# A shared PSUM bank in the gated-linear-attention scan: keys in halves of it, products in the attention's ring

## The chip, the cores and the metric

The kernel runs on one core of a Trainium2 chip. The metric is the device time of one execution in microseconds (us); lower is better.

## The reference, cut to what matters

A two-layer backbone over 1280 tokens (256 context, then 1024 latent) of width 1024. Each layer normalises its input, multiplies it by one input projection, runs three groups of heads on the result and adds one output projection of them all:

```python
for layer in range(DEPTH):            # DEPTH = 2
    p = h @ w_in                      # one combined input projection
    gdn = gdn_branch(...)             # gated DeltaNet, a scan over chunks
    mla = mla_branch(...)             # softmax attention, 8 heads, 96-wide keys
    gla = gla_branch(...)             # gated linear attention, a scan over chunks
    x = x + gate * (concat([gdn, mla, gla]) @ w_out)
```

The change sits in the last branch, the gated linear attention (GLA), in its recurrence over chunks, run once forward and once backward over the tokens:

```python
o = (qi * jnp.exp(bi)) @ state + scores @ vi
state = state * jnp.exp(b_last)[..., None] + einsum(ki * jnp.exp(b_last - bi), vi)
```

## The kernel before, in words

The kernel is one program in the Tile language. It is written as a sequence of instructions; a planner of the language then lists each engine's instructions in an order that it works out with a timeline of its own (`schedule_with_timeline_sim=True`), gives tiles their buffers and adds the waits. A pool with `bufs=n` has n buffers for a tag: a new tile takes one whose earlier tile has been read for the last time, and its first writer waits for that reader.

In each layer, after the projections, `run` starts two strands of work and interleaves them. The foreground is first `up` (the attention's queries, keys and values), then `attend`. The background is a generator: the scan of the gated DeltaNet (`gdn_scan`), then `gla_prep`, seven levels `gla_level` and at last `gla_scan`. After each step of the foreground one step of the background is written.

`attend` works in units: one tile of 128 queries against all 1280 keys of one head. Scores go to tiles `sa` (two banks each, two buffers) and `sb`; ScalarE takes exponentials; ten 128x128 transposes (`ptr`, L1243) bring the probabilities into tiles of the tag `t`, four, four and two at a time, and ScalarE or VectorE copies each to SBUF (L1247). For each group of four units `output` multiplies with the values into a tile `O` (40 matmuls, L1255, and four with the reciprocal sums, L1267), also of the tag `t`, and VectorE reads it (L1269, L1271). The tag `t` has two buffers, each a PSUM bank: this is the attention's ring.

The background has one PSUM bank of its own, tag `l`, one buffer. The helper that hands out both:

```python
def g(self, name="g", tag="g"):
    if tag == "l":
        return self.psl.tile([128, 512], F32, name=name, tag=tag, bufs=1)
    return self.ps.tile([128, 512], F32, name=name, tag=tag, bufs=self.psb[tag])
```

`gla_scan` has ten stages `st`, each with both directions `d`. A stage transposes two 128x128 key tiles into a tile `kdt` (L950), which ScalarE copies to `ktl` (L952); multiplies queries with the state and the scores with the values into `gO` (L961, L964), which ScalarE or VectorE brings to `oL` (L973, L975); and multiplies the keys with the values into `gF` (L980), from which VectorE makes the new state `Sl` with a mask (L982) and the decayed old state (L988). `kdt` and `gF` exist in the first nine stages of each layer; `gO` in all ten of the first layer and in eight of the second, which needs no output for the context: 18 tiles of each name in all. `Sl` and `ktl` have two buffers. After stages 1, 7 and 9 `head_norm` norms and gates finished outputs and writes them to DRAM (`y_d`, L1009).

When the background is done its SBUF pools close, and `proj_start` lays its pool `yC` over the same memory: it loads the attention's output (`yst`, L1316) and the first output weights (`wost`, L248, split by L249 and L250 with one staging buffer), makes gate tiles (L1331, tag `l`) and transposes the scans' outputs (`ytr`, L1350). `proj` then loads the other weights over the attention's memory and runs the output projection (`po`).

Of the kernel before, what the change touches and what calls it, by code (L numbers as in the profile page):

```python
# [43 lines left out]
class Net:  # L44
# [25 lines left out]

    def S(self, name="S"):
        return self.ps.tile([128, 1536], F32, name=name, tag="S", bufs=self.psb["S"])

# [130 lines left out]
    def h_stage(self, l, a, b):  # L204
# [17 lines left out]
        for k in range(8):  # L222
            if k % 2 == 0:
                pp = self.S("hps")
            ps = pp[:, 512 * (k % 2):512 * (k % 2) + w]
# [33 lines left out]
    def chan(self, w, j, lo=0):  # L259

        hi, lw = (t.rearrange("p (k n) -> p k n", k=8) for t in w)
        ps = self.S("pin")
        for c0, cn in CHUNKS:
# [419 lines left out]
    def gdn_scan(self, l):  # L683
# [7 lines left out]
        oS = sp.tile([128, 20 * 256], F32, name="oS", tag="oS", bufs=1)  # L691
        S = None
        lanes = [(d, h) for h in range(4) for d in range(2)]
# [7 lines left out]
        for s in range(20):  # L701
# [23 lines left out]
            r = vt  # L725
            if S is not None:
                pk = self.g("kS", "l")
# [198 lines left out]
    def gla_scan(self, l):  # L926
        nc, sp = self.nc, self.sp
        last = l == L - 1
        mm = nc.tensor.matmul
        V, A, P = nc.vector, nc.scalar, nc.gpsimd  # L930
        Q, K, tot = (self.lst[n] for n in ("Q", "K", "tots"))

        def at(i):

            return self.A5[i // 2][:, 512 * (i % 2):512 * (i % 2) + 512]

        oL = [self.bp.tile([128, 512], F32, name="oL", tag="oL", bufs=5) for _ in range(5)]
        order = (tuple(range(10)), (1, 0) + tuple(range(9, 1, -1)))
        S = [None, None]
        for st in range(10):  # L940
            vs, kt = [], None
            for d in range(2):
                vv = sp.tile([128, 256], F32, name="gvt", tag="gvt", bufs=4)
                nc.sync.dma_start(vv, self.gv_d[l][order[d][st]])
                vs.append(vv)
            if st < 9:
                pk = self.g("kdt", "l")
                for d in range(2):
                    i = order[d][st]
                    nc.tensor.transpose(pk[:, 128 * d:128 * d + 128], K[d][:, 128 * i:128 * i + 128], self.ident)  # L950
                kt = sp.tile([128, 256], F32, name="ktl", tag="ktl", bufs=2)
                A.copy(kt, pk[:, 0:256])  # L952
                yield
            todo = [d for d in range(2) if not (last and order[d][st] < CT) and (d == 0 or S[d] is not None)]
            if todo:
                ps = self.g("gO", "l")
                for d in todo:
                    i = order[d][st]
                    pd = ps[:, 256 * d:256 * d + 256]
                    if S[d] is not None:  # L960
                        mm(pd, Q[d][:, 128 * i:128 * i + 128], S[d], start=True, stop=(d == 1))  # L961
                    if d == 0:
                        for hd in range(4):
                            mm(pd[:, 64 * hd:64 * hd + 64], at(i)[:, 128 * hd:128 * hd + 128], vs[0][:, 64 * hd:64 * hd + 64],  # L964
                               start=(S[d] is None), stop=(S[d] is None or hd == 3))
                for d in todo:
                    i = order[d][st]
                    o = oL[i // 2][:, 256 * (i % 2):256 * (i % 2) + 256]
                    pd = ps[:, 256 * d:256 * d + 256]

                    other = (1 - i if i < 2 else 11 - i) if d == 0 else i
                    if st < other or (d == 0 and i == 1):
                        A.copy(o, pd)  # L973
                    else:
                        V.tensor_tensor(o, pd, o, ALU.add)  # L975
                yield
            if st < 9:
                pf = self.g("gF", "l")
                for d in range(2):
                    mm(pf[:, 256 * d:256 * d + 256], kt[:, 128 * d:128 * d + 128], vs[d], start=True, stop=True)  # L980
                Sn = sp.tile([128, 512], F32, name="Sl", tag="Sl", bufs=2)
                V.tensor_tensor(Sn.rearrange("p (d n) -> p d n", d=2), pf.rearrange("p (d n) -> p d n", d=2),  # L982
                                self.bdm.unsqueeze(1).broadcast_to([128, 2, 256]), ALU.mult)
                for d in range(2):
                    Sd = Sn[:, 256 * d:256 * d + 256]
                    if S[d] is not None:
                        i = order[d][st]
                        V.scalar_tensor_tensor(Sd, S[d], tot[:, d, i:i + 1], Sd, ALU.mult, ALU.add)  # L988
                    S[d] = Sd
            for j in {1: (0,), 7: (2, 3), 9: (1, 4)}.get(st, ()):  # L990
                self.head_norm(l, 1, oL[j], j)
            yield
# [591 lines left out]
```

## Time and profile before

| | us |
|---|---|
| runs shown: lowest, median, highest of 3 | 2273.74, 2279.19, 2281.04 |
| the profiled execution, its own time | 2280.18 |
| its span, first to last instruction | 2278.4 |
| mean granted TensorE clock | 0.946 of full |

The first layer's attention begins some 640 us into the span and its GLA scan some 954 us; in the second layer the scan begins some 2043 us. PE is TensorE's matmuls, DVE is VectorE, ACT is ScalarE, POOL is GpSimd, SPq is SyncE's queue of DMA issues.

### The profile page before, as it was taken

The page shows a single profiled execution, that of the slowest core. Times are in us where ns is not written, and L with a number is a line of the kernel's source. Part 1 is how long each engine was busy: PE and PEld are TensorE (multiplying, and loading weights), DVE is VectorE, ACT ScalarE, POOL GpSimd, SP SyncE. Part 2 cuts the span into 40 slices and gives each one's busy share as a digit, 9 for nine tenths or more (in the row PEclk, how much of TensorE's full clock was granted, in tenths as well). Part 3 has the DMA queues.
Part 4 walks back from the last instruction along what each step waited for, and adds up shares of the span by engine and source line. Part 5 has one row for each costly group of instructions (what it writes and reads, how often), then busy time and mean ns, then how long its engine had stood idle before and what let it go on. Part 6 is the DMA issues. An engine that isn't in the chain of part 4 may idle for free.

```text
span 2278.4 us, 44490 instructions
## 1 busy us (share of the span) xinstructions
PE 2043.3 (90%) x17820; PEld 1709.8 (75%) x17820; DVE 1291.6 (57%) x2187; ACT 941.1 (41%) x1926; POOL 743.7 (33%) x936
## 2 busy tenths in 40 slices
PE   5998997999989988898897998976987999899998
PEld 3987896886767766676897987875876776667688
DVE  3446685323447689656425356795233677975634
ACT  3246311533235466555204356212542445564531
POOL 1233265122234543214103322381123264421410
PEclk8999998899989999999898999998998999899999
DMA  7111343258742231113424212424266242101352
GB/s 296 47 62 61 105 119 113 84 200 284 220 109 76 76 111 36 40 48 121 161 93 171 65 36 81 136 69 115 90 197 168 58 115 96 54 24 50 100 155 103
DMA packets 207551, 247.34 MB, mean 109 GB/s; under 512 B 60976, under 2 KB 164464, under 8 KB 203760
## 3 DMA queue, kind: packets, MB, share of 16 engines
q1 hardware_dynamic: 207344, 244.49, 34.1%
q8 instruction: 140, 2.29, 0.4%
q14 instruction: 67, 0.55, 0.1%
HBM read 168.14 MB, written 76.28 MB: 107 GB/s over the span
## 4 chain that ended last, share of the span: by engine, by line
PE 46%; DVE 13%; ACT 5%; DMA 5%; issue 3%; POOL 2%; SPq 1%; DVEq 0%; POOLq 0%; ACTq 0%
PE O L1255 6%; PE ptr L1243 4%; PE po L257 3%; PE po L255 3%; PE po L256 3%; PE sa L255 3%; PE sa L256 2%; PE sa L257 2%; PE ptk L255 1%; PE ptk L256 1%; PE ptk L257 1%; DVE XT L634 1%; DVE X L636 1%; PE kS L730 1%; DVE acc L345 1%
## 5 line engine op out<-in xcount | busy, mean ns | idle before, releaser
L255 PE MATMUL ptk<-whi,hhi 128*128 128x256 f32 (+1 forms) x912 | 263.6, 290 | 6.1 <-DVE ev L297 2.2
L257 PE MATMUL ptk<-whi,hlo 128*128 128x256 f32 (+1 forms) x912 | 261.9, 288 | 1.8 <-POOL hlo L238 1.7
L256 PE MATMUL ptk<-wlo,hhi 128*128 128x256 f32 (+1 forms) x912 | 261.7, 287 | 0.4 <-DVE wlo L250 0.4
L1243 PE MATMUL ptr<-c_id,P 128*128 128x128 f32 x1312 | 203.6, 283 | 27.8 <-ACT PT L1247 18.8
L1243 PEld LDWEIGHTS ptr<-c_id,P 128*128 128x128 f32 x1312 | 151.2, 143 | 78.1 <-ACT PT L1247 29.9
L1247 ACT COPY PT<-ptr 128x512 f32<-128x512 f32 (+1 forms) x256 | 122.3, 480 | 211.1 <-PE ptr L1243 209.7
L256 PE MATMUL pin<-hlo,whi 128*128 128x512 f32 (+1 forms) x544 | 201.6, 371 | 1.6 <-issue 1.6
L255 PE MATMUL pin<-hhi,whi 128*128 128x512 f32 (+1 forms) x544 | 202.5, 372 | 0.0
L257 PE MATMUL pin<-hhi,wlo 128*128 128x512 f32 (+1 forms) x544 | 201.8, 372 | 0.0
L255 PEld LDWEIGHTS ptk<-whi,hhi 128*128 128x128 f32 x912 | 179.4, 197 | 10.8 <-issue 4.3
L1206 DVE TENSOR_REDUCE mx<-sa 128x1 f32<-128x1024 f32 x128 | 156.2, 1220 | 53.6 <-PE sa L257 53.0
L257 PEld LDWEIGHTS ptk<-whi,hlo 128*128 128x128 f32 x912 | 178.8, 197 | 5.3 <-POOL hlo L238 3.0
L256 PEld LDWEIGHTS ptk<-wlo,hhi 128*128 128x128 f32 x912 | 179.4, 197 | 3.1 <-issue 2.0
L1255 PE MATMUL O<-PT,vv 128*64 128x256 f32 x1312 | 169.6, 388 | 1.7 <-ACT PT L1247 0.9
L255 PE MATMUL po<-wohi,yh 128*128 128x256 f32 x576 | 164.4, 286 | 4.4 <-DVE yl L1353 2.1
L256 PE MATMUL po<-wolo,yh 128*128 128x256 f32 x576 | 164.0, 285 | 0.0
L257 PE MATMUL po<-wohi,yl 128*128 128x256 f32 x576 | 162.6, 285 | 0.0
L1228 ACT ACTIVATE P<-sa,mx 128x1024 f32<-128x1024 f32 x128 | 142.2, 1111 | 0.0
L1255 PEld LDWEIGHTS O<-PT,vv 128*64 128x64 f32 x1312 | 97.2, 138 | 59.0 <-issue 11.9
L255 PE MATMUL sa<-kTh,qTh 128*128 128x512 f32 (+1 forms) x272 | 118.3, 436 | 21.1 <-ACT kTh L1152 15.2
L250 POOL TENSOR_TENSOR wlo<-wst,whi 128x1024 fp32r<-128x1024 f32 x32 | 84.1, 2639 | 127.5 <-ACT whi L249 126.4
L256 PEld LDWEIGHTS pin<-hlo,whi 128*128 128x128 f32 x544 | 105.6, 194 | 19.7 <-issue 4.4
(341 smaller groups left out, 5030.6 us busy)
## 6 DMA issues: line engine op xcount, KB each, us to landing
wada<-in_w_ada_dram SPq DMA_DIRECT2D x24, 1024.0 KB
wst<-in_w_in_dram SPq DMA_DIRECT2D x48, 512.0 KB
kv<-ktv_d SPq DMA_DIRECT2D x80, 128.0 KB
wost<-in_w_out_dram SPq DMA_DIRECT2D x16, 512.0 KB
xt<-in_x_all_dram SPq DMA_DIRECT2D x10, 512.0 KB
at_d<-D SPq DMA_DIRECT2D x4, 1280.0 KB
kn_d<-uo SPq DMA_DIRECT2D x20, 256.0 KB
v_d<-uo SPq DMA_DIRECT2D x20, 256.0 KB
```

The lines of the kernel that those rows point to most:

```text
L250: E.tensor_tensor(lo[:, h], st, hi[:, h].bitcast(F32), ALU.subtract)
L255: mm(out, lh, rh, start=first, stop=False)
L256: mm(out, lh, rl, start=False, stop=False)
L257: mm(out, ll, rh, start=False, stop=last)
L345: nc.vector.scalar_tensor_tensor(a, raw[:, tap:tap + 1282], cw[:, ti, tap:tap + 1], a, ALU.mult, ALU.add)
L634: E.tensor_tensor(tmp, Xv[B, G, 0:k, k].unsqueeze(3).broadcast_to([q, n, nr, ncl]), Xv[B, G, k, k + 1:32].unsqueeze(2).broadcast_to([q, n, ...
L636: E.tensor_tensor(dst, dst, tmp, ALU.add)
L1206: V.tensor_reduce(mx[:, 0:1], sas[u], AX.X, ALU.max, negate=True)
L1228: A.activation(p[:, 0:1024], ta, AF.Exp, bias=mx[:, 0:1], accum_out=r[:, 0:1])
L1243: nc.tensor.transpose(tp[:, 128 * (k - ka):128 * (k - ka) + 128], p[:, 128 * c:128 * c + 128], self.ident)
L1247: (V.tensor_copy if ka == 4 else A.copy)(PT[hh][:, ka:kb, 128 * (i % 2):128 * (i % 2) + 128], tp[:, 0:128 * (kb - ka)].rearrange("p (k t) ...
L1255: mm(po[64 * h2:64 * h2 + 64, 0:256], vv[m][:, 128 * k + 64 * h2:128 * k + 64 * h2 + 64], PT[h2][:, k, :], start=(k == 0), stop=(k == nk - 1))
```

## The change

The tile `kdt` is taken once for the whole scan, and successive stages use its left and right half in turn. The tiles `gO` and `gF` come from the tag `t`, the two banks that the attention's `ptr` and `O` tiles use.

```diff
         S = [None, None]
+        W = self.g("kdt", "l")
         for st in range(10):
...
             if st < 9:
-                pk = self.g("kdt", "l")
+                pk = W[:, 256 * (st % 2):256 * (st % 2) + 256]
                 for d in range(2):
                     i = order[d][st]
                     nc.tensor.transpose(pk[:, 128 * d:128 * d + 128], K[d][:, 128 * i:128 * i + 128], self.ident)
                 kt = sp.tile([128, 256], F32, name="ktl", tag="ktl", bufs=2)
-                A.copy(kt, pk[:, 0:256])
+                A.copy(kt, pk)
                 yield
...
             if todo:
-                ps = self.g("gO", "l")
+                ps = self.g("gO", "t")
...
             if st < 9:
-                pf = self.g("gF", "l")
+                pf = self.g("gF", "t")
```

## Rows read from the trace of the kernel before

**Rows 1.** The page's busy times: engine, us (share of the span), instructions.
```profile
PE 2043.3 (90%) x17820; PEld 1709.8 (75%) x17820; DVE 1291.6 (57%) x2187; ACT 941.1 (41%) x1926; POOL 743.7 (33%) x936
```
**Rows 2.** Windows: stretch, its length, busy us of each engine, granted clock, DMA share.
```profile
840.00:950.00 110.00, 95.78 (x842) 66.02 (x842) 93.63 (x175) 67.36 (x160) 36.65 (x56) 0.94 0.14 40
954.00:1052.00 98.00, 94.89 (x617) 74.80 (x616) 63.44 (x125) 49.65 (x127) 23.88 (x31) 1.00 0.18 55
2043.00:2138.00 95.00, 93.45 (x618) 73.13 (x616) 57.79 (x115) 47.16 (x116) 20.26 (x25) 1.00 0.18 55
1058.00:1108.00 50.00, 36.48 (x235) 28.67 (x234) 24.03 (x49) 24.66 (x46) 23.34 (x19) 0.86 0.65 212
1076.00:1091.00 15.00, 6.01 (x27) 4.58 (x26) 3.31 (x7) 7.83 (x15) 9.14 (x6) 0.65 0.86 289
2140.00:2190.00 50.00, 42.48 (x314) 33.38 (x313) 20.95 (x46) 24.94 (x51) 25.09 (x22) 1.00 0.53 163
2140.00:2152.00 12.00, 10.92 (x72) 8.01 (x72) 10.26 (x23) 7.75 (x20) 6.74 (x8) 1.00 0.25 71
```
**Rows 3.** Timeline of PE in the first scan: start, us, instruction, idle before.
```profile
954.15 0.38 PE L950 MATMUL kdt<-c_id,KK 128*128 128x128 f32 x2
...
988.68 0.44 PE L950 MATMUL kdt<-c_id,KK 128*128 128x128 f32 x2 [0.40 <-DVE Sl L982]
...
991.81 0.59 PE L961 MATMUL gO<-Sl,QQ 128*128 128x256 f32 x2
...
994.46 1.13 PE L980 MATMUL gF<-gvt,ktl 128*128 128x256 f32 x4
...
997.80 0.38 PE L950 MATMUL kdt<-c_id,KK 128*128 128x128 f32 x2
...
1038.62 0.44 PE L950 MATMUL kdt<-c_id,KK 128*128 128x128 f32 x2
...
1049.67 0.59 PE L961 MATMUL gO<-Sl,QQ 128*128 128x256 f32 x2
```
**Rows 4.** Waits of PE, 954 to 1052 us: us in total, times, longest.
```profile
PE kdt L950 <- DVE Sl L982: 0.4, 1, 0.4
```
**Rows 5.** Waits of PE, 640 to 954 us, the attention before the scan.
```profile
PE ptr L1243 <- ACT PT L1247: 4.4, 9, 1.8
PE ptr L1243 <- DVE PT L1247: 3.3, 5, 1.6
```
**Rows 6.** Timeline of ACT, the scan of the first layer and the attention after the second.
```profile
993.76 0.65 ACT L973 COPY oL<-gO 128x256 f32<-128x256 f32 x2 [2.76 <-PE gO L961]
...
2147.26 0.59 ACT L1247 COPY PT<-ptr 128x512 f32<-128x512 f32 x1
```
**Rows 7.** Timeline of DVE in the first scan.
```profile
995.63 0.69 DVE L982 TENSOR_TENSOR Sl<-gF,c_bdm 128x512 f32<-128x512 f32 x1 [2.40 <-PE gF L980]
```
**Rows 8.** Timeline of PE, attention after each layer's scan.
```profile
1053.13 4.54 PE L1255 MATMUL O<-PT,vv 128*64 128x256 f32 x40
...
1059.55 0.85 PE L1243 MATMUL ptr<-c_id,P 128*128 128x128 f32 x6 [0.51 <-DVE ym L1271]
...
2141.04 1.58 PE L1243 MATMUL ptr<-c_id,P 128*128 128x128 f32 x10
...
2145.03 1.50 PE L1243 MATMUL ptr<-c_id,P 128*128 128x128 f32 x10
```
**Rows 9.** The chain that ended last, 1055 to 1080 us: start, us, what.
```profile
1061.85 0.36 SPq L1009
...
1063.26 5.45 DMA wost<-in_w_out_dram
...
1072.24 3.83 DMA wost<-in_w_out_dram
```
**Rows 10.** Timeline of PE, the first layer's change from attention to output projection.
```profile
1080.69 0.69 PE L1350 MATMUL ytr<-c_id,yx 128*128 128x128 f32 x2 [4.21 <-ACT gate L1332]
...
1090.43 0.56 PE L255 MATMUL po<-wohi,yh 128*128 128x256 f32 x1
```

## The prediction

> **What bounds the kernel now.** I read the page first: TensorE's matmuls are busy 90% of the span and no other engine comes near [rows 1]. An average over stages says little about one of them, so next come the windows around the change. In both scans PE is busy 94.89 of 98 us and 93.45 of 95, at full clock [rows 2]: 3.1 and 1.6 us of idle time are all that any edit inside these stretches can take away. The list of PE's waits then asks how much of this is owed to the shared bank: one wait of the keys' transposes for the state's evacuation, 0.4 us [rows 4]. The bank makes the background slow, but PE has the attention to do meanwhile.
>
> How slow, the timeline shows. In the first layer the keys are transposed nine times between 954.15 and 1038.62, a stage every 10.6 us. One stage has three legs of similar length: keys at 988.68, output at 991.81, state at 994.46, the next keys at 997.80 [rows 3]. Each leg is one tile going through the one bank.
>
> The last view is of what follows. The background's last product is at 1049.67 [rows 3]; the write of its normed output is issued at 1061.85, and only then, in memory that it frees, do the output weights come, in pieces 9 us apart (1063.26, 1072.24) [rows 9]. The attention ends soon after, and PE waits: 4.2 us for a gate tile whose copy stands behind casts of loaded data, and the projection begins at 1090.43 [rows 10]. In 1058 to 1108 PE idles 13.5 us at a clock of 0.86, and in 1076 to 1091 it is busy 6.0 of 15 us. In the second layer, where the scan ends earlier against the attention, the like stretch 2140 to 2190 idles 7.5 us at full clock [rows 2]. So a scan that ends earlier is worth something, at that place alone.
>
> **The change part by part.** No instruction is added or taken away, and no DMA; what moves is which tile waits for which.
>
> *Keys in halves of their own bank.* The wait of 0.4 us goes [rows 4]: -0.4. The keys no longer stand behind the state's evacuation; the nearest thing they wait for is their own copy a stage before, long done. So of the three legs the one from state to keys (3.3 us in the stage shown) falls out, and the one from keys to output (3.1) leaves the chain, since the output needs no new keys [rows 3]. What is late next is the state: product, mask, decay, then the next output; I allow it two legs of about 3.5 us with waits for a bank. A stage then takes some 7 to 7.5 us, and nine stages end 25 us earlier (0 if the legs were PE's turn and not the bank's; 40 if hardly anything binds).
>
> *Products in the ring.* This adds 36 tiles, 18 `gF` and 18 `gO`, to two banks. What does the ring carry today? Transposes come every 4.0 us in attention alone (2141.04, 2145.03 [rows 8]); their tiles are held from 2145.03 to the end of the last copy at 2147.85 [rows 6, 8], so at most 2 x 2.8 = 5.6 bank-us per unit. An `O` tile is held from 1053.13 to 1059.55, where transposes wait 0.51 us for its release [rows 8]: 6.4 us for four units, 1.6 each. Together at most 7.2 of 8.0 bank-us. A `gO` is held from 991.81 to 994.41, a `gF` from 994.46 to 996.32 [rows 3, 6, 7]: 4.5 bank-us a stage. PE spends at most 3.6 us on a stage (0.44 for keys, 1.95 up to the first copy of `gO`, 1.17 up to the mask), so a stage of 7.6 us leaves time for one unit: 7.2 + 4.5 = 11.7 of 15.2 bank-us. The ring is no fuller than in attention alone; but its tiles come less evenly. A wait of the transposes for an evacuation costs today 7.7 us / 14 = 0.55 us [rows 5]. Below, none of the 36 tiles causes one, since PE has scores and keys to put there: 0. Above, each does: +20. I take one in four, as PE is full here and the tile's holder has its own work on PE: +5. Queued behind a waiting product or transpose on PE are the next scores, and behind these the maxima on DVE and the exponentials on ACT.
>
> A clock that falls would cost more than the idle time itself. The rows say that it holds where PE is kept busy (1.00 in both scans) and is 0.94 in 840 to 950, where PE idles 14 us of 110 [rows 2]. The Trainium skill, "TensorE: Matmul & The Clock Gate", section "A second HAM failure mode: psum-queue depth-cycling", says that cycling through PSUM banks with small idle gaps between groups of matmuls makes the clock swing between its two levels, 1.2 and 2.4 GHz. By the rows of the scan the sum has nothing for it; by that rule it would be the fourth rival's.
>
> *The time after the scan.* Attention alone idles 1.08 us of 12, 9%, against 2 to 3% with the scan [rows 2]. Where 25 us more of it stand at the end of each layer: 2 x 25 x 6.6% = +3.3 (0 to 5).
>
> *The change to the projection.* With 25 us in hand the first weights, the gates and the first transposes lie before the attention's end. The rest of the weights goes into the attention's memory and can't come earlier. I take the second layer's stretch as what remains in the first: 13.5 - 7.5 = 6 us of idle time, and about 3 us for the clock (0.86 against 1.00 over 36.5 busy us is 5 at most). In the second layer most is hidden already: 2. Together -11; bounds 0 (other loads bind) and -20 (all of 13.5, the 3, and half of 7.5).
>
> *Sum:* -0.4 + 5 + 3.3 - 11 = -3.1. The profiled execution took 2280.2 us, 1.8 more than its span, and 1.0 more than the median of the runs. So 2277.1 on its scale, 2276 on that of the runs. A difference below 0.3%, 6.8 us, can hardly be told from none here.
>
> **The rivals.**
> 1. *The ring's waits hide and the scan ends early.* For it: 97 to 98% of a scan's time is PE's own work, and the demand on the ring isn't above today's. Against it: two banks for four kinds of tile. With no ring waits, 14 us won at the projection and 1.5 lost to attention alone: -0.4 - 14 + 1.5 = -13, 2266 us.
> 2. *The transposes starve.* A `gF` can be made ahead, but its mask writes a state buffer (two of them) that the output before must have read: both banks then hold the background's tiles while the attention's transposes wait, and scores fill only two `sa`. Place: the scans. Price: once a stage the part of a `gF`'s hold beyond its own PE time, 1.9 - 1.0, 18 times, 16 us; the scan then ends less early, so half the gain: 16 + 3 - 5.5 - 0.4 = +13, 2292 us. It decides from about 14 us of PE waits for the ring in the two scans on (11 - 3.3 + 6.8).
> 3. *The background isn't faster.* PE lists the background's tiles between runs of the attention's, and the legs may be its turn rather than the bank. Then -0.4 and a few ring waits: 2280 us. For it: PE idles but once, 0.4 us, for the bank in the first scan [rows 4], so most of a leg may be a queue. Against it: a stage has as many legs as the bank has tiles, and they are alike [rows 3].
> 4. *The clock falls in the scans.* At 0.94 as in 840 to 950, 6% of 193 us is 11.6 us on top of the forecast: 2288 us. For it: small waits of PE are what the change adds. Against it: attention alone, with 9% of idle time, has 1.00 [rows 2]. The skill's section on depth-cycling speaks for it.
>
> **How the numbers follow.** Chances: forecast 0.30, rival 1 0.30, rival 2 0.20, rival 3 0.12, rival 4 0.08. Faster by over 0.3% is rival 1: 0.30. Within 0.3%: the forecast and rival 3, 0.42. Slower: rivals 2 and 4, 0.28. The bounds of the terms give -0.4 - 20 and +20 + 5, or 2259 to 2304; leaving out a tenth at each end, 2261 to 2296. The forecast alone, with rival 3: 2272 to 2285.
>
> **What would show it.** Right: in the profile after, keys come at no fixed distance from the states; a stage takes 7 to 8 us; the first layer's last `gO` is near 1025 and the first output weights are loaded some 25 us earlier; PE in the scans idles 3 to 6% by waits of `ptr` for copies and for `Sl` or `oL`; the stretch after the attention's end has PE idle 7 us and not 13.5. Wrong: a stage still of 10 us, so that the bank was not the pace; waits of `ptr` for `Sl` or `oL` above 14 us in the two scans; a granted clock below 1.00 there; or a projection that begins 14 us after the attention's end though its first weights came early, so that other loads bind. The planner lists all later instructions anew, so differences of a few us can come from places that the change doesn't touch.

## The result and the profile after

The changed kernel takes 2489.03 us, median of 4 runs (2480.22 to 2491.34), against 2279.16: a ratio of 1.0918, 95% interval 1.0886 to 1.0950. It is 210 us slower, where I had forecast no change, with a range up to 2296 us (the bounds of my terms reached 2304).

The page of the changed kernel, its busy times and two lines of its 40 slices, shows at once that something other than a crowded ring has happened:

```profile
PE 2090.8 (84%) x17820; PEld 1747.4 (70%) x17820; DVE 1293.3 (52%) x2187; ACT 942.4 (38%) x1926; POOL 739.8 (30%) x936
...
PE   5998978999764589999897998968978546899998
...
PEclk7999989999865599999998999989989557999999
```

Against [rows 1] PE has 211.1 us more of span: 47.5 more of busy time, in which the same 17820 instructions took longer, and 163.6 more of idle time. There are two holes, one in each layer, with the clock near half. In the windows of these holes (stretch, length, busy us of each engine, granted clock, DMA share, GB/s)

```profile
704.00:850.00 146.00, 66.33 (x1030) 52.09 (x1026) 79.07 (x156) 37.85 (x77) 57.05 (x70) 0.52 0.14 47
1930.00:2084.00 154.00, 70.57 (x1017) 55.05 (x1013) 79.49 (x147) 33.91 (x65) 61.49 (x73) 0.51 0.14 47
```

no engine is busy for more than 54% of the time, and PE idles 79.7 and 83.4 us. The waits of PE from 700 to 870 us, of the changed kernel (total, times, longest), name only the background's tiles:

```profile
PE gsc L874 <- DMA KK<-gqk_d: 18.9, 1, 18.9
PE gsc L874 <- DVE A L879: 15.4, 12, 2.4
PE gsc L874 <- ACT A L885: 12.6, 2, 6.7
PE Tr L740 <- DVE r L733: 10.3, 6, 3.5
```

What is missing says more than what is there. The timeline of PE in the changed kernel, those rows that belong to the attention's ring and the keys:

```profile
694.57 0.38 PE L1244 MATMUL ptr<-c_id,P 128*128 128x128 f32 x2
...
850.69 1.97 PE L965 MATMUL gO<-gvt,A 128*128 128x64 f32 x8
...
863.73 0.69 PE L951 MATMUL kdt<-c_id,KK 128*128 128x128 f32 x2 [1.39 <-ACT A L896]
864.88 2.08 PE L981 MATMUL gF<-gvt,ktl 128*128 128x256 f32 x4 [0.46 <-ACT ktl L953]
866.75 1.06 PE L1244 MATMUL ptr<-c_id,P 128*128 128x128 f32 x4
...
868.03 1.06 PE L962 MATMUL gO<-Sl,QQ 128*128 128x256 f32 x2
...
870.49 0.60 PE L1244 MATMUL ptr<-c_id,P 128*128 128x128 f32 x4
...
871.57 1.13 PE L981 MATMUL gF<-gvt,ktl 128*128 128x256 f32 x4 [0.27 <-DVE oL L976]
...
1200.62 0.56 PE L255 MATMUL po<-wohi,yh 128*128 128x256 f32 x1
...
1921.60 0.66 PE L1244 MATMUL ptr<-c_id,P 128*128 128x128 f32 x4
...
2083.00 2.07 PE L981 MATMUL gF<-gvt,ktl 128*128 128x256 f32 x4 [0.46 <-ACT ktl L953]
2084.87 0.63 PE L1244 MATMUL ptr<-c_id,P 128*128 128x128 f32 x2
...
2388.19 0.39 PE L255 MATMUL po<-wohi,yh 128*128 128x256 f32 x1
```

From 694.57 to 866.75 the attention makes no transpose at all: it stands still for 172 us, and in the second layer from 1921.60 to 2084.87, 163 us. In this time the background goes on alone through the gated DeltaNet's scan and the GLA levels. When it has done its first `gO` and its first `gF` (in the second layer, whose first two stages have no `gO`, its first `gF`), the transposes start again, and from there on ring tiles of the two strands take turns. The scan's first keys come at 863.73 and not 954.15 [rows 3], but the attention has all the rest of its work before it: the output projection begins at 1200.62, not 1090.43 [rows 10], 110 us later. The second layer's projection begins at 2388.19, not 2171.16, 217 us later.

Theory 1: the two banks of the ring are handed out in the order in which the tiles are *written*. The background's steps are written one after each of the attention's, so its first `gO` stands some 58 steps into the attention's 450, after about nine of 72 units. It *runs* much later, since the background is slow. In the kernel before that cost nothing: the strands shared no buffer and the attention went on ahead. In the changed kernel all transposes written after that `gO` stand behind it. The rows fit: from 850.69 on PE takes `gO`, `gF`, four transposes, `gO`, four transposes, `gF`, which is the order in which the kernel writes these tiles. Theory 2, closest to my prediction: the 36 tiles crowd two banks. Theory 3: the key tile held through the scan, or a plan that came out badly.

### The profile page after: what moved, and what is told of

It reads as the page before. It is cut to its first block, busy times and chain, and to the rows that moved or that the text cites. A ratio compares the mean times of both kernels' runs of the same rounds, so it can differ in the third digit from the quotient of the medians.

```text
span 2489.5 us, 44624 instructions
## 1 busy us (share of the span) xinstructions
PE 2090.8 (84%) x17820; PEld 1747.4 (70%) x17820; DVE 1293.3 (52%) x2187; ACT 942.4 (38%) x1926; POOL 739.8 (30%) x936
## 4 chain that ended last, share of the span: by engine, by line
PE 46%; DVE 12%; DMA 5%; issue 4%; ACT 4%; POOL 3%; SPq 1%; DVEq 0%; POOLq 0%; ACTq 0%
PE O L1256 6%; PE ptr L1244 5%; PE po L256 2%; PE po L257 2%; PE po L255 2%; PE sa L255 2%; PE sa L256 2%; PE sa L257 2%; PE ptk L255 2%; PE ptk L257 2%; PE ptk L256 1%; PE gsc L874 1%; PE kS L730 1%; DVE XT L634 1%; PE pin L256 1%
## 5 line engine op out<-in xcount | busy, mean ns | idle before, releaser
L1256 PE MATMUL O<-PT,vv 128*64 128x256 f32 x1312 | 154.6, 384 | 1.1 <-ACT PT L1248 0.5
```

The source lines that it names most:

```text
L1256: mm(po[64 * h2:64 * h2 + 64, 0:256], vv[m][:, 128 * k + 64 * h2:128 * k + 64 * h2 + 64], PT[h2][:, k, :], start=(k == 0), stop=(k == nk - 1))
```

## The experiments

Each is compared with the kernel before in runs on the same chip (its median is 2284.87 us for one tile, the late scan, its control and half way, and 2280.53 for the other four).

**One tile.** In the kernel before, only the first `gO` of each layer goes to the ring.

```diff
-                ps = self.g("gO", "l")
+                ps = self.g("gO", "l" if once else "t")
+                once = True
```

> The kernel before, but the first gO of each layer's scan, and it alone, takes a bank of the attention's ring; keys, all other gO and all gF stay in the background's bank. Theory 1 (the ring's banks are handed out in the order in which the tiles are written, so attention transposes written after the first gO can't start before the whole background up to it is done): the attention stands still as long as with all 36 tiles, 170 us per layer, and the time is 2460 to 2510 us. Theory 2 (36 more tiles crowd two banks): 2 of 36 tiles, a loss of some 12 of 210 us, 2280 to 2295. Theory 3 (halves of a tile held through the scan, or a plan that came out badly): none of it is in this kernel, 2270 to 2290.

Measured: 2468.81 us, ratio 1.0796 (1.0758 to 1.0833). Two of the 36 tiles, one in each layer, bring 184 of the 210 us, so it isn't the number of tiles that costs. The timeline of PE in this kernel has the same hole, which ends as soon as this `gO` is done:

```profile
694.19 0.38 PE L1245 MATMUL ptr<-c_id,P 128*128 128x128 f32 x2
...
848.79 1.97 PE L966 MATMUL gO<-gvt,A 128*128 128x64 f32 x8
850.55 1.06 PE L1245 MATMUL ptr<-c_id,P 128*128 128x128 f32 x4
```

The transposes begin at 850.55, before ScalarE's copy that empties the tile's bank, which begins at 850.79: they weren't waiting for that bank, but stood behind its products in PE's order. The run also shows part of what the other tiles add: here transposes return at 850.55, in the changed kernel 16 us later, behind `gF` as well.

**The same place, a tile that is ready.** The kernel before, with an extra tile of the ring where the last run had its `gO`: a transpose of a constant and a copy that nothing reads.

```diff
+            if st == (2 if last else 0):
+                px = self.g("gX", "t")
+                nc.tensor.transpose(px[:, 0:128], self.ident, self.ident)
+                A.copy(self.ap.tile([128, 128], F32, name="dum", tag="dum", bufs=1), px[:, 0:128])
```

> The kernel before plus one extra tile of the attention's ring per layer, written where the run with one gO had its tile, but with nothing to wait for: a transpose of the constant identity and a ScalarE copy of it that nothing reads. gO stays in the background's bank. Theory 1 (the ring's order ties the attention to the background's progress because the tile taken isn't ready): this tile is ready at once, so no standstill and 2270 to 2295 us. Theory 2 (any tile of the background in the ring costs the attention): about 2469, as with one gO.

Measured: 2284.96 us, ratio 1.0014 (0.9992 to 1.0035): no loss that can be told. In the timeline of PE it takes its turn at 693.30, where the holes of the last run and of the changed kernel begin, and the transposes follow 0.17 us later:

```profile
693.30 0.33 PE L956 MATMUL gX<-c_id 128*128 128x128 f32 x1
693.47 0.60 PE L1247 MATMUL ptr<-c_id,P 128*128 128x128 f32 x4
...
696.80 0.44 PE L1247 MATMUL ptr<-c_id,P 128*128 128x128 f32 x2
```

The window of the hole, 146 us long, has PE busy for 132.14 us at a clock of 0.97 here. A background tile in the ring did no harm where it could run in its written place.

**The scan written later.** The changed kernel with all its ring tiles, but the scan's steps are held back to the attention's step 338 of 450 (295 of 398 in the second layer), where the scan ran in the kernel before:

```diff
+                    while self.att < LATE[l]:
+                        yield
                     yield from self.gla_scan(l)
...
+                self.att = 0
                 for _ in self.attend(l):
+                    self.att += 1
...
```

> The changed kernel with all its ring tiles, but the GLA scan's steps are written later, from the attention's step 338 of 450 on (295 of 398 in the second layer), about where the scan ran in the kernel before. Theory 1: attention is no longer behind the background, the standstill is gone and the time is 2260 to 2300 us; the ring's real crowding, which I had put at +5, and the earlier end of the scan show here. Theory 2: the same tiles in the same banks beside the same attention, 2440 to 2490. Theory 3 leaves the loss as well if the halves made it.

Measured: 2296.29 us, ratio 1.0053 (1.0034 to 1.0072). The same 36 tiles, the same halves, the same banks, and 95% of the loss is gone. The control, the same edit in the kernel before, with the scan's tiles in the background's own bank:

> Control: the kernel before, with the GLA scan written as late as in the run beside it, all its tiles in the background's own bank. Theory 1: this bank never tied the two strands, so the time stays at 2270 to 2290 us; what the run beside it differs by is the ring's alone. Theory 2: the same, no change. Were the written place itself of weight (which of two ready instructions the planner lists first), it would show here.

Measured: 2302.18 us, ratio 1.0073 (1.0044 to 1.0101): the place alone costs some 17 us, which I had not expected. Most of it is at the end of the second layer, where the attention's last product begins at 2166.5 and the projection at 2189.1, after a wait of 12.2 us for ScalarE's cast of the turned outputs. The late kernel with the ring is 6 us faster than this control; that is below 0.3%, but all its nine runs (2293.01 to 2300.06) lie under all four of the control (2301.05 to 2306.05).

**Half way.** The same edit with steps 200 and 177, and the ring:

> The changed kernel, the scan written from the attention's step 200 of 450 on (177 of 398), between the changed kernel (58) and the late one (338). Theory 1: the attention stops at that step, some 190 us into it, when the background is about to begin its GLA levels, which alone take some 90 us; about 45 us lost per layer, 2340 to 2410 us. Theory 2: as the changed kernel, 2440 to 2490.

Measured: 2378.95 us, ratio 1.0403 (1.0362 to 1.0443). In its timeline of PE the attention now stops later and for half as long, 88 us:

```profile
821.00 0.66 PE L1245 MATMUL ptr<-c_id,P 128*128 128x128 f32 x4
...
893.26 1.97 PE L966 MATMUL gO<-gvt,A 128*128 128x64 f32 x8
...
909.31 0.63 PE L1245 MATMUL ptr<-c_id,P 128*128 128x128 f32 x2
```

Steps 58, 200 and 338 give 210, 94 and 11 us of loss: the loss goes with the distance between where the tile is written and where it is ready.

**Whole key tiles.** The changed kernel without the halves:

```diff
-                pk = W[:, 256 * (st % 2):256 * (st % 2) + 256]
+                pk = self.g("kdt", "l")[:, 0:256]
```

> The changed kernel without the halves: each stage's keys take a new tile of the background's bank, as before; gO and gF in the ring. Theory 1: the halves have no part in the loss and hardly one in anything, 2470 to 2500 us. Theory 3 (the tile held through the scan is to blame): near 2280.

Measured: 2486.67 us, ratio 1.0882 (1.0845 to 1.0918). The interval overlaps that of the changed kernel: the halves have no part in the loss that can be told from none, and theory 3's held tile falls. So does its plan that came out badly: four kernels with separate plans (the changed one, one tile, half way, whole keys) stop where the scan's first ring tile is written. The halves don't set the scan's pace either: in the first layer the keys come every 4.3 us with whole tiles (nine between 856.65 and 890.83) and with halves (863.73 to 898.50).

**Spread out.** The late kernel, from steps 318 and 284, one step of the scan after every second or third step of the attention.

```diff
-                    yield from self.gla_scan(l)
+                    for _ in self.gla_scan(l):
+                        for _ in range(2):      # 3 in the other run
+                            yield
```

> The changed kernel with the scan written late (from step 318 and 284) and then one of its steps after every second step of the attention, not each. With one step after each, the ring's strict order crowded the scan into 64 us, PE idled 6.6 us there and the attention then ran 70 us without a filler. Theory 1 with the ring's order as the pace: the scan spreads over some 58 steps, PE stays as busy as in the kernel before and the time falls to 2270 to 2290 us. If the loss of the late kernel were crowding of the banks, it stays at 2290 to 2300.

> As the run before it, one step after every third step of the attention: 29 steps over 87, to step 405 of 450. Theory 1: PE full to near the end, but the output weights come as late as in the kernel before: 2272 to 2292 us. Crowding: 2290 to 2300.

Measured: 2285.01 us, ratio 1.0010 (0.9993 to 1.0026), and 2283.07 us, ratio 1.0007 (0.9987 to 1.0026). With the written places spread over the time in which the scan can run, the ring costs nothing that can be told from none, and it wins nothing. PE isn't as full as I had expected of the second of them: busy 82.22 of 90 us in 955 to 1045. I found no version that beats the kernel before.

## Why the prediction was wrong

*The step that failed* is "Products in the ring". I took what a tile costs the ring to be the time that it holds a bank, 4.5 bank-us a stage, and put the sum beside the ring's capacity; the term was +5 with a bound of +20. The runs showed another cost in its place: the order in which a ring's banks are handed out. A tile holds up the later ones from the place where it is written until it is ready, whether or not it holds a bank, and that was a standstill of 156 and 170 us in the two layers with one tile, and of 172 and 163 us with all of them. The facts for it stood in my own views. The scan's steps are written early in the attention, a step after a step, and [rows 3] have it run from 954 to 1050, near the attention's end. I read this lag as the background's slowness and not as a lead of the attention that the separate bank alone allowed. I took for granted that a free bank goes to whichever tile is ready; nothing in my account of the kernel said in which order a pool serves the tiles that ask.

*The side rival, transposes that starve*, had the right victim and the wrong reason: it priced a hold of 1.9 us in the scans at 16 us. The transposes starved before the scan began, behind a tile that held nothing yet.

*Its place.* I looked only at the scan's windows and at what follows them. The loss is in windows that hold no instruction of the edited lines, 704 to 850 us. What my text named as a test, waits of `ptr` for `Sl` or `oL` above 14 us, doesn't show it either, because the waits are put down to the instruction that is next in PE's order: the transposes were listed behind the background's products, and it is these that wait.

*The clock.* Rival 4 had it falling in the scans. With the strands uncoupled, in the late kernel with the ring, the windows of the two scans read:

```profile
955.00:1019.00 64.00, 57.36 (x348) 45.17 (x346) 39.16 (x77) 25.41 (x67) 17.74 (x21) 0.97 0.19 58
...
2046.00:2122.00 76.00, 67.31 (x425) 53.20 (x424) 45.59 (x87) 34.15 (x85) 18.13 (x20) 0.99 0.19 52
```

These are 0.97 and 0.99 where PE idles 6.6 and 8.7 us among short waits: below the 1.00 that I had named, so that the sign of this rival is there, but above the 0.94 that I priced. Read in stretches of 8 us, the clock fell once in each scan (0.79 in 955 to 963 and in 2118 to 2126) and was 1.00 in all the others. The Trainium skill's section on depth-cycling ("TensorE: Matmul & The Clock Gate", "A second HAM failure mode: psum-queue depth-cycling") describes a bf16 kernel whose clock swings between its levels as it cycles through PSUM banks. The trace of this ring, with fp32 operands, shows one short fall in each scan and no swinging. The clock did fall to 0.52 and 0.51, almost all the time at the lower of its two levels, 1.2 GHz, but in the standstill, where PE was busy 66 us of 146. That made the standstill longer, as the background's own products ran at half speed: eight of `gsc` (L893) take 1.97 us there and 1.08 us at full clock in the kernel before.

*The other terms* can be read from the late kernel against its control. These differ by the whole change, ring and halves, but by the run with whole key tiles the halves add nothing to the pace. Rows of PE: the first and last `gO` of the first scan, for the ring and then (second fence) for the bank.

```profile
968.09 1.00 PE L966 MATMUL gO<-gvt,A 128*128 128x64 f32 x8
...
1016.60 0.70 PE L963 MATMUL gO<-Sl,QQ 128*128 128x256 f32 x2 [0.40 <-DVE Sl L990]
```

```profile
953.51 1.00 PE L965 MATMUL gO<-gvt,A 128*128 128x64 f32 x8
...
1048.89 0.59 PE L962 MATMUL gO<-Sl,QQ 128*128 128x256 f32 x2
```

- The shared bank was the scan's pace: a stage takes 5.4 us with the ring and 10.6 with the bank. I had 7 to 7.5. The scan ends 32 us earlier, in both layers (1018.2 against 1050.4, 2121.4 against 2153.7); I had 25.
- The change to the projection gains. In the first layer the projection begins 8.1 us after the start of the attention's last product, at 1098.60 after 1090.5, against 22.9 in the control (1092.4 after 1069.5) and 15.8 in the kernel before (1090.4 after 1074.6); in the second 0.3 against 22.6 and 0.8. Against the kernel before that is 8 and 0.5 us; I had 9 and 2.
- Ring waits and attention alone cost more than +5 and +3.3. In the late kernel PE idles 15.3 us in the two scans against 4.7 in the kernel before [rows 2], and 16.6 in the 141 us of attention after them against 6.7 in 56 us. In the first layer the attention ends 21 us later than in the control. Of the gain against the control 6 us are left.

So the sum of these terms, near zero, would have come near for a kernel whose scan is written where it runs: 1.0007 to 1.0053 in the three such runs. For this one it left out the term that decides.

*What isn't settled.* That banks are handed out in written order is inferred from the runs: the place alone and the readiness alone each move the time as it says, and neither of the other two theories fits both. Whether the planner's list of PE's instructions or its choice of a bank holds the later tiles back was not taken apart; with one tile the transposes weren't waiting for its bank (850.55 against 850.79), which speaks for the list. The 26 us between two tiles and 36 are shown in part, by the 16 us of the first layer. Why the place alone costs the control 17 us is seen in its second layer but was not tried by a run.

## What to carry to other kernels

A private buffer between two strands of work is not only capacity: it lets one run ahead of the other. Before tiles of a slow strand go into the ring of a fast one, look up where each is written and where it runs in the trace; the difference, not the time that the tile holds its buffer, is what the fast strand can lose. If they must share, write the slow strand's steps where they will be ready, and test it with one tile.

## What the runs showed that I had not expected

One tile of one bank per layer cost 184 us, and a tile in the same place that was ready cost none (1.0014, 0.9992 to 1.0035). The background gained less than I would have thought from having the chip to itself: from the start of the hole at 694.57 its first `gO` came after 156 us, against some 261 beside the attention in the kernel before (850.69 against 955.60), while from 704 to 850 us, with PE at a clock of 0.52, no engine was busy more than 79 us of 146.
